# Splitting the first modulation unit of a two-layer transformer kernel into one half per chunk of the input

## Chip, cores, metric

One core of one Trainium2 chip runs the whole program. The metric is the device time of one execution in microseconds (us). Before the change three runs gave 2346.82, 2341.54 and 2345.47; the median is 2345.47 us.

## What is computed

The reference is a two-layer model on 512 latent rows and 256 context rows of width 2048, in float32. What matters here is its very beginning, the modulated norm that feeds layer 0:

```
shift, scale, gate = jnp.split((sc @ ada_w[i] + ada_b[i])[:, None, :], 3, axis=-1)
shift_c, scale_c, gate_c = jnp.split(scc @ ada_w[i] + ada_b[i], 3, axis=-1)
h = rmsnorm(x, norm_w[i]) * (1.0 + scale) + shift
hc = rmsnorm(xc, norm_w[i]) * (1.0 + scale_c) + shift_c
...
p_in, p_gate, c_q, c_kv, k_r, a_gate = split_cols(h @ w_in, EV_SIZES)
```

`sc` and `scc` are the SiLU of two vectors of length 2048, and `ada_w[i]` is 2048 x 6144. So before the first product `h @ w_in` can start, two things have to be there: the row norms of x (a sum of squares over all 2048 columns), and the shift and scale of the columns in question (a product with 2048 rows of `ada_w`).

## The kernel before

**Layout.** x and the context lie transposed: 16 chunks `xt[j]` of 128 columns (on the partitions) by 768 rows (512 latent, 256 context). Each float32 product is made of three products of split operands, high by high, low by high and high by low, with `wh`, `wl` the two parts of a weight and `h0h`, `h0l` those of an activation.

**First norm (L363 to L377).** SyncE issues the loads of all 16 chunks. ScalarE squares a chunk (L369, L372), VectorE adds it to one running sum `ssq0` (L374, 14 additions; the tile's name is `rb0`). Then TensorE sums over the partitions: `stat_mm` makes six one-column matmuls for `ssq0` and six for the last square `sq` (L375, L376, helper L247). `rstd_col` (L221 to L225) makes the reciprocal root, `rows` (L239 to L241) spreads it over the partitions: six diagonal tiles `dg`, six matmuls into `prs`, and two copies into `rb0`.

**Modulation units.** A unit `u` is 512 columns of `ada_w` for two chunks: in units 0 to 7 the columns are the shift of chunks 2u and 2u+1, then their scale. `ada_steps` (L134) works a unit off in steps. Each of four steps loads two tiles `at` of 512 KB and makes four matmuls into one PSUM tile `pa`, each with 32 columns of weights into its own 32 rows of `pa` (the trace shows each of them as two, so a step is x8). After the fourth VectorE transposes `pa` into `ga` (L147); a small matmul `pb` sums the parts (L150); four additions on VectorE write shift and scale into `av` (L131).

**A chunk.** `h_chunk` (L258) needs `av` and `rb0`. VectorE makes the factor `acf` (L264) and the product `ht` (L269), ScalarE the high part `h0h` (L271), VectorE the low part `h0l` (L272); first for the 512 latent rows, then for the 256 context rows. Each chunk then feeds five entries of a work list: four pairs (group g, block b), each six matmuls `px` (L360, 512 columns) and `pc` (L361, 256 columns) in alternation, and one of three matmuls `gkr` (L358).

**Order of the work.** TensorE runs in the order in which the code is written (`manual_schedule`); the other engines' order is set by the scheduler of the framework. The loop over e = 0 to 7 (L400) takes chunks 2e and 2e+1. From e = 1 on, the steps of unit e stand between entries of the work list by a table: after each step as many entries (`main_step`) as `PLAN = (0, 2, 3, 3, 2)` says. With ten entries in the list, the products of chunks 2e-2 and 2e-1 lie among the steps of unit e. The weight tiles come by `load_w` (L111) and `load_kr` (L389) every second e; all loads stand in one queue on SyncE. The `at` tiles share 11 buffers. When the loop is over, the evacuation and the next norm follow (L447 to L462), and from there on units 8 and up are worked off by VectorE, ScalarE and GpSimd beside the matmuls.

In PSUM the small tiles (`ps6`, `pa`, `prs`, `pb`) alternate between two banks. From L384 on one of the two holds `gkr`, and `pa` and `pb` of all later units share the other.

Of the kernel before, what the change touches and what calls it, by code (L numbers as in the profile page):

```python
# [29 lines left out]
V_GB, V_SINK, V_PS, V_QN, V_KVN, V_HN, V_FN, V_NW, V_AB = 0, 16, 32, 36, 40, 44, 52, 68, 132  # L30
# [8 lines left out]
def tile_hybrid_dit(ctx: ExitStack, tc: tile.TileContext, ts: dict, out: bass.AP, dbg=None, upto=99):  # L39
    nc = tc.nc  # L40
    T, V, S, G, DM = nc.tensor, nc.vector, nc.scalar, nc.gpsimd, nc.sync
# [44 lines left out]
    cst = opool(ctx, "cst")  # L86
    st = cst.tile([P, KC, 32], F32, name="st")
# [5 lines left out]
    vec = cst.tile([P, V_N], F32, name="vec")  # L93
# [31 lines left out]
    def ada_place(u, pb, n):  # L125
# [5 lines left out]
            V.tensor_tensor(a[sl, :, :n], pb[:, :n, b4::4].rearrange("p v b -> p b v"), ab[:, :, :n], op=ALU.add)  # L131
        av[u] = a

    def ada_steps(u, pp, tp, nb=3, nt=2):  # L134

        pa = pp.tile([P, 512], F32, name=f"pa{u}", tag="pm")
        for q in range(4):
            at = []
            for i in range(2):
                at.append(tp.tile([P, 2, 512], F32, name=f"at{u}_{q}_{i}", tag="ada", bufs=nb))  # L140
                DM.dma_start(at[i], ts["ada"][u, 2 * q + i].rearrange("p (k w) -> p k w", w=512))
            for qd in range(4):
                T.matmul(pa[32 * qd : 32 * qd + 32, :], st[:, 4 * q + qd, :], at[qd // 2][:, qd % 2, :],
                         start=q == 0, stop=q == 3, skip_group_check=True)
            if q == 3:
                tr = tp.tile([P, 16, 32], F32, name=f"ga{u}", tag="ga", bufs=1)
                V.transpose(tr.rearrange("p b r -> p (b r)"), pa)  # L147
                yield
                pb = pp.tile([32, 2, 16], F32, name=f"pb{u}", tag="pm")
                T.matmul(pb, fold, tr[:, :, 0:2].rearrange("p b v -> p v b"), start=True, stop=True)  # L150
                ada_place(u, pb, 2)
            yield
# [91 lines left out]
    def stat_mm(ps6, sq, nb, d, first=True, last=True):  # L244
        col = onesd[d]
        for b in range(nb):
            T.matmul(ps6[:, b : b + 1], sq[:, b * P : (b + 1) * P], col,  # L247
                     start=first and b == 0, stop=last and b == nb - 1, skip_group_check=True)
# [9 lines left out]
    def h_chunk(j, xt, rb, u0, layer, hh, hl, tp, vs=(0, 1), low=V):  # L258

        a = av[u0 + j // 2]  # L260
        i = j % 2
        nw = vec[:, V_NW + 32 * layer + 2 * j : V_NW + 32 * layer + 2 * j + 2]
        ac = tiny.tile([P, 2], F32, name="acf", tag="acf", bufs=2)
        V.scalar_tensor_tensor(ac, a[:, 2 + i, :], 1.0, nw, op0=ALU.add, op1=ALU.mult)  # L264
        n0 = PARTS[vs[0]].start
        t = tp.tile([P, PARTS[vs[-1]].stop - n0], F32, name="ht", tag="ht")
        for v in vs:
            sl = slice(PARTS[v].start - n0, PARTS[v].stop - n0)
            V.scalar_tensor_tensor(t[:, sl], xt[:, PARTS[v]], ac[:, v : v + 1], rb[v], op0=ALU.mult, op1=ALU.mult)  # L269
            if low is V:  # L270
                S.activation(hh[v], t[:, sl], AF.Identity, bias=a[:, i, v : v + 1], scale=1.0)  # L271
                V.scalar_tensor_tensor(hl[v], t[:, sl], a[:, i, v : v + 1], hh[v], op0=ALU.add, op1=ALU.subtract)  # L272
            else:
                S.activation(t[:, sl], t[:, sl], AF.Identity, bias=a[:, i, v : v + 1], scale=1.0)
                S.copy(hh[v], t[:, sl])
                low.tensor_tensor(hl[v], t[:, sl], hh[v], op=ALU.subtract)

# [57 lines left out]
    pp = ppool(esP, "ppA", px=4, pc=2, pm0=1, pm1=1)  # L335
# [13 lines left out]
    ae = opool(esE, "adaE", side="right")  # L349
# [14 lines left out]
    ps6 = pp.tile([P, 6], F32, name="ps6", tag="pm", bufs=2)  # L364
    ssq0 = sp.tile([P, NT], F32, name="rb0")
    for j in range(KC):
        DM.dma_start(xt[j], ts["xT"][j])
    NB, FIRST = 11, 2
    S.activation(ssq0, xt[0], AF.Square)  # L369
    for j in range(1, KC):  # L370
        sq = sp.tile([P, NT], F32, name="sq", tag="ht", bufs=2)
        S.activation(sq, xt[j], AF.Square)  # L372
        if j < KC - 1:
            V.tensor_tensor(ssq0, ssq0, sq, op=ALU.add)  # L374
    stat_mm(ps6, ssq0, 6, D, True, False)  # L375
    stat_mm(ps6, sq, 6, D, False, True)  # L376
    r6 = rstd_col(ps6, 6)  # L377
    first_unit = ada_steps(0, pp, ae, NB)
    for _ in range(FIRST):
        next(first_unit)  # L380
    rb0 = rows(r6, 6, pp, ssq0)
    for _ in first_unit:
        pass
    gx = [new_px(2) for _ in range(2)]  # L384
    gc = [new_pc() for _ in range(2)]
# [9 lines left out]

    wq = {}
    EARLY = 4
    PLAN = (0, 2, 3, 3, 2)
    with tc.manual_schedule(engines={mybir.EngineType.PE}):
        ht = Ring(sp, 2)  # L400
        for e in range(8):
            if e % 2 == 0:
                for g in range(2):
                    wq[g] = load_w(win[g, e // 2])
                wq[2] = load_kr(e // 2)
            if e:
# [63 lines left out]
    for kq in range(2):  # L470
        w = load_w(ts["ev_kr"][kq], 1024, 128)
# [77 lines left out]
    for pr in range(2):  # L549
# [11 lines left out]
        for b in range(2):  # L561
            t = ta("psg")
# [20 lines left out]
    pp = ppool(esP, "ppM", s2=2, pj=2, pm=2)  # L583
# [205 lines left out]
    first = out0_first()  # L789
# [90 lines left out]
    pp = ppool(esP, "ppO", px=4, pc=2, pm=2)  # L880
# [94 lines left out]
    for kq in range(8):  # L975
        w = load_w(ts["od_mv0"][kq], 544, 272)
# [740 lines left out]
def pack(inputs):  # L1717
# [8 lines left out]
    for l in range(2):  # L1726
        w = f["ada_w"][l]
        b = f["ada_b"][l]
        for e in range(8):
            cols = np.r_[256 * e : 256 * e + 256, 2048 + 256 * e : 2048 + 256 * e + 256]  # L1730
            ada.append((w, b, cols))
        for e in range(4):
            ada.append((w, b, np.r_[4096 + 512 * e : 4096 + 512 * e + 512]))
# [98 lines left out]
```

## Time and profile before

| | |
|---|---|
| median of three runs | 2345.47 us |
| the profiled execution, its own time | 2345.14 us |
| its span in the trace | 2343.4 us |
| TensorE busy (matmul) | 2238.1 us, 96% of the span |
| VectorE busy | 1488.9 us, 64% |
| ScalarE busy | 1041.4 us, 44% |
| first matmul at | 23.94 us |
| first product of a chunk (`px`) at | 41.82 us |
| end of the last `gkr` product of the loop | about 156.5 us |

A row of the timeline has the start in us, the time from the first to the end of the last of a run of like instructions, the engine, the line, the operation, output and input with shapes, and how many. In square brackets stands how long the engine had been idle and what ended it. PE is TensorE's matmul, PEld its weight load, DVE VectorE, ACT ScalarE, POOL GpSimd, SPq the queue of loads that SyncE issues.

### The profile page before, as it was taken

Reading aid. Unit: us, or ns where it says so; the run is one execution under the profiler, and the core shown is the slowest. Engines: PE = TensorE matmul, PEld = TensorE weight load, DVE = VectorE, ACT = ScalarE, POOL = GpSimd, SP = SyncE. Lnnn points to the kernel's source line nnn. Section 1 sums busy time; section 2 is a strip of 40 time slices with the busy share of each in tenths; the row PEclk is TensorE's granted clock in tenths of the full one; section 3 lists DMA queues with packets and bytes.
Section 4 is the critical chain, followed back from the end, with each engine's and each line's share of the span. In section 5 each row is a group of like instructions: output and inputs, shape, how many; then the busy total and the mean of one; then the engine's idle time right before and its main releaser. Section 6 shows DMA issues by size and latency. Waiting matters only on the chain.

```text
span 2343.4 us, 34744 instructions
## 1 busy us (share of the span) xinstructions
PE 2238.1 (96%) x12920; PEld 1902.8 (81%) x12920; DVE 1488.9 (64%) x2748; ACT 1041.4 (44%) x2054; POOL 459.0 (20%) x393
## 2 busy tenths in 40 slices
PE   5999998999999999999999999999999999999997
PEld 3678887778889999877888898998888877777886
DVE  5578888875476666777767722522555576778435
ACT  4234454443244444554224522222655557666433
POOL 0015565764200000026212200000000010003111
PEclk9999999999999999999999999999999999999998
DMA  9854554563311111255775322123233212113434
GB/s 383 323 197 161 171 185 140 202 205 123 99 57 48 59 52 64 91 186 198 241 248 178 116 95 82 64 73 114 99 99 97 99 62 72 64 55 126 135 113 140
DMA packets 118586, 311.27 MB, mean 133 GB/s; under 512 B 13676, under 2 KB 21356, under 8 KB 118416
## 3 DMA queue, kind: packets, MB, share of 16 engines
q1 hardware_dynamic: 111536, 281.73, 35.9%
q0 software_dynamic: 6880, 27.32, 3.0%
q8 instruction: 101, 1.65, 0.3%
q14 instruction: 69, 0.57, 0.1%
HBM read 279.37 MB, written 29.62 MB: 132 GB/s over the span
## 4 chain that ended last, share of the span: by engine, by line
PE 68%; DVE 9%; issue 4%; DMA 3%; POOL 2%; ACT 2%; DVEq 0%; SPq 0%; ACTq 0%; POOLq 0%
PE px L289 20%; PE px L302 11%; PE pj L619 5%; PE pc L291 5%; PE px L1418 5%; PE s L682 4%; PE pc L302 3%; PE om L725 3%; PE pj L639 2%; POOL acc L169 2%; DMA at<-in_ada_dram 2%; PE s L1418 2%; DVE acc L164 2%; PE po L1337 2%; DVE wl L109 2%
## 5 line engine op out<-in xcount | busy, mean ns | idle before, releaser
L109 DVE TENSOR_TENSOR wl<-wraw,wh 128x512 fp32r<-128x512 f32 (+2 forms) x556 | 431.9, 783 | 420.3 <-ACT wh L108 417.1
L108 ACT CAST wh<-wraw 128x512 fp32r<-128x512 f32 (+2 forms) x556 | 324.5, 589 | 594.7 <-PE pc L291 145.9
L169 POOL TENSOR_TENSOR acc<-acc,at 128x512 f32<-128x512 f32 x180 | 282.7, 1571 | 282.7 <-ACT at L167 272.9
L164 DVE SCALAR_TENSOR_TENSOR acc<-at,st,acc 128x512 f32<-128x512 f32 x240 | 250.3, 1043 | 52.1 <-DMA at<-in_ada_dram 48.3
L167 ACT ACTIVATE at<-at,st 128x512 f32<-128x512 f32 x180 | 130.0, 724 | 180.2 <-DVE acc L164 152.8
L302 PE MATMUL px<-wh,hxh 128*128 128x512 f32 (+2 forms) x512 | 174.4, 341 | 0.1
L302 PE MATMUL px<-wl,hxh 128*128 128x512 f32 (+2 forms) x512 | 173.7, 339 | 0.0
L302 PE MATMUL px<-wh,hxl 128*128 128x512 f32 (+2 forms) x512 | 173.6, 339 | 0.0
L289 PE MATMUL px<-h0h,wl 128*128 128x512 f32 x384 | 155.3, 404 | 11.7 <-DVE wl L109 11.7
L289 PE MATMUL px<-h0h,wh 128*128 128x512 f32 x384 | 156.0, 406 | 1.0 <-ACT wh L108 0.8
L289 PE MATMUL px<-h0l,wh 128*128 128x512 f32 x384 | 153.7, 400 | 0.0
L291 PE MATMUL pc<-h0h,wl 128*128 128x256 f32 x400 | 113.9, 285 | 0.0
L291 PE MATMUL pc<-h0h,wh 128*128 128x256 f32 x400 | 113.7, 284 | 0.0
L291 PE MATMUL pc<-h0l,wh 128*128 128x256 f32 x400 | 113.6, 284 | 0.0
L302 PEld LDWEIGHTS px<-wh,hxh 128*128 128x128 f32 x512 | 96.2, 188 | 12.8 <-ACT sz L1261 1.0
L302 PEld LDWEIGHTS px<-wl,hxh 128*128 128x128 f32 x512 | 96.3, 188 | 11.3
L302 PEld LDWEIGHTS px<-wh,hxl 128*128 128x128 f32 x512 | 96.2, 188 | 11.0
L289 PEld LDWEIGHTS px<-h0h,wl 128*128 128x128 f32 x384 | 73.5, 191 | 32.2 <-DVE wl L109 15.5
L289 PE MATMUL px<-zxh,wl 128*128 128x512 f32 x224 | 88.9, 397 | 3.6 <-DVE wl L109 3.6
L289 PE MATMUL px<-zxh,wh 128*128 128x512 f32 x224 | 89.6, 400 | 2.0 <-ACT wh L108 1.1
L289 PEld LDWEIGHTS px<-h0h,wh 128*128 128x128 f32 x384 | 73.9, 193 | 19.5 <-ACT wh L108 2.5
L289 PE MATMUL px<-hxl,wh 128*128 128x512 f32 x224 | 89.2, 398 | 0.0
(877 smaller groups left out, 6231.7 us busy)
## 6 DMA issues: line engine op xcount, KB each, us to landing
at<-in_ada_dram SPq DMA_DIRECT2D x256, 256.0 KB, 3.1
at<-in_ada_dram SPq DMA_DIRECT2D x64, 512.0 KB, 8.2
wraw<-in_od_in_dram SPq DMA_DIRECT2D x64, 512.0 KB, 3.5
wraw<-in_ev_in_dram SPq DMA_DIRECT2D x56, 512.0 KB, 4.1
wraw<-in_ev_out_dram SPq DMA_DIRECT2D x44, 512.0 KB, 4.5
wraw<-in_od_out_dram SPq DMA_DIRECT2D x36, 512.0 KB, 3.5
wraw<-in_od_oz_dram SPq DMA_DIRECT2D x32, 512.0 KB, 3.5
xt<-in_xT_dram SPq DMA_DIRECT2D x16, 384.0 KB, 7.5
```

The costliest lines, as they stand in the source:

```text
L108: S.copy(h, src)
L109: low.tensor_tensor(l, src, h, op=ALU.subtract)
L164: V.scalar_tensor_tensor(acc[0], at, st[:, kc, 0:1], acc[0], op0=ALU.mult, op1=ALU.add)
L167: S.mul(m, at, st[:, kc, 1:2])
L169: G.tensor_tensor(acc[1], acc[1], m, op=ALU.add)
L289: T.matmul(px[b], w_, Hx[kc][r_], start=s0, stop=s1)
L291: T.matmul(pc[b], w_, Hc[kc][r_], start=s0 and b == 0, stop=s1, skip_group_check=True)
L302: T.matmul(p_, h_, w_, start=s0, stop=s1, skip_group_check=True)
L619: T.matmul(t, w_, r_[:, sl], start=kc == 0 and n == 0, stop=kc == 3 and n == 2)
L682: T.matmul(s[:, c0 - k0 : c1 - k0], l_, r_[:, c0:c1], start=n == 0, stop=n == 4)
L725: T.matmul(o[:, :256], v_[:, 6 - nk + b, :], p_[:, b, :], start=b == 0 and n == 0, stop=b == nk - 1 and n == 2)
L1418: T.matmul(px[b], w_, Hs[kc][r_], start=first and i == 0 and n == 0, stop=last and i == len(kcs) - 1 and n == 2)
```

## The change

Four edits, all at the beginning of the program:

1. The first norm's running sum is cut into three parts. At chunk 5 and chunk 10 the sum so far goes through its six `stat_mm` matmuls, and a new sum begins with a copy of the square on VectorE; the last part, with the last square added, goes last. That makes 13 additions and 2 copies where 14 additions were, and 18 one-column matmuls where 12 were.
2. The columns of units are packed so that chunk 2u's shift and scale stand first, then those of chunk 2u+1. Unit 0 is worked off in two halves by the new `ada_half_steps`: each half has eight loads of 256 KB (rows of 1 KB where rows of 4 KB were), four steps of matmuls 256 columns wide, a transpose of 256 columns, a `pb`, and four additions into its half of `av[0]`.
3. Half 0 stands where the whole unit stood. Half 1 stands ahead of `h_chunk` of chunk 1, and the five work entries of chunk 0 are issued ahead of half 1 (`main_step` five times right after chunk 0 is made).
4. `PLAN` becomes (2, 2, 2, 2, 2). At e = 1 the list holds only chunk 1's five entries.

```diff
+    def ada_half_steps(u, hf, pp, tp, nb):
+        pa = pp.tile([P, 512], F32, name=f"pa{u}_{hf}", tag="pm")[:, :256]
+        for q in range(4):
+            at = []
+            for i in range(2):
+                at.append(tp.tile([P, 2, 512], F32, name=f"at{u}_{hf}_{q}_{i}", tag="ada", bufs=nb)[:, :, :256])
+                DM.dma_start(at[i], ts["ada"][u, 2 * q + i].rearrange("p (k w) -> p k w", w=512)[:, :, 256 * hf : 256 * hf + 256])
+            for qd in range(4):
+                T.matmul(pa[32 * qd : 32 * qd + 32, :], st[:, 4 * q + qd, :], at[qd // 2][:, qd % 2, :],
+                         start=q == 0, stop=q == 3, skip_group_check=True)
+            yield
+        tr = tp.tile([P, 8, 32], F32, name=f"ga{u}_{hf}", tag="gah", bufs=1)
+        V.transpose(tr.rearrange("p b r -> p (b r)"), pa)
+        pb = pp.tile([32, 2, 8], F32, name=f"pb{u}_{hf}", tag="pm")
+        T.matmul(pb, fold, tr[:, :, 0:2].rearrange("p b v -> p v b"), start=True, stop=True)
...
     for j in range(1, KC):
         sq = sp.tile([P, NT], F32, name="sq", tag="ht", bufs=2)
         S.activation(sq, xt[j], AF.Square)
-        if j < KC - 1:
-            V.tensor_tensor(ssq0, ssq0, sq, op=ALU.add)
-    stat_mm(ps6, ssq0, 6, D, True, False)
-    stat_mm(ps6, sq, 6, D, False, True)
+        if j in (5, 10):
+            stat_mm(ps6, acc, 6, D, first, False)
+            acc, first = su.tile([P, NT], F32, name="sqs", tag=f"sqs{j}"), False
+            V.tensor_copy(acc, sq)
+        else:
+            V.tensor_tensor(acc, acc, sq, op=ALU.add)
+    stat_mm(ps6, acc, 6, D, False, True)
+    esU.close()
     r6 = rstd_col(ps6, 6)
-    first_unit = ada_steps(0, pp, ae, NB)
-    for _ in range(FIRST):
-        next(first_unit)
+    halves = [ada_half_steps(0, hf, pp, ae, NB) for hf in range(2)]
+    for _ in range(2):
+        next(halves[0])
     rb0 = rows(r6, 6, pp, ssq0)
-    for _ in first_unit:
+    for _ in halves[0]:
         pass
...
-    PLAN = (0, 2, 3, 3, 2)
+    PLAN = (2, 2, 2, 2, 2)
...
             for j in (2 * e, 2 * e + 1):
+                if j == 1:
+                    for _ in halves[1]:
+                        pass
                 h_chunk(j, xt[j], [rb0[:, p] for p in PARTS], 0, 0, *([H0[j][i][:, p] for p in PARTS] for i in range(2)), ht)
...
+                if j == 0:
+                    for _ in range(5):
+                        main_step()
```

From the end of the loop on, the order on every engine is the same as before. Three places on TensorE are the ones that the prediction speaks of. The names: `pa<-at` is a step of a unit or half, `pb<-ga` its last small matmul, `prs` belongs to the row norms; the activations are numbered, `h0h_161` and `h0l_162` are chunk 0, 163 and 164 chunk 1, 165 and 166 chunk 2.

First, the way to the first product of chunk 0. Before, the last step of unit 0, then two steps of unit 1 (`pa_406`) ahead of the product:

```order
L143 MATMUL pa_289<-at_3_1_338,st 32x512 x2
L240 MATMUL prs<-dg,con 128x128 x2
L150 MATMUL pb_346<-ga_344,con 32x32
L143 MATMUL pa_406<-at_0_0_407,st 32x512 x2
L143 MATMUL pa_406<-at_0_1_409,st 32x512 x2
L143 MATMUL pa_406<-at_1_0_415,st 32x512 x2
L143 MATMUL pa_406<-at_1_1_417,st 32x512 x2
L360 MATMUL px<-h0h_161,wh 128x512
```

After the change, at the same place, nothing stands between the `pb` of half 0 (`pb_0`) and chunk 0:

```order
L143 MATMUL pa_0_302<-at_0_3_1_351,st 32x256 x2
L264 MATMUL prs<-dg,con 128x128 x2
L149 MATMUL pb_0_359<-ga_0_357,con 32x16
L384 MATMUL px<-h0h_161,wh 128x512
L385 MATMUL pc<-h0h_161,wh 128x256
```

The two steps of unit 1 have moved behind chunk 0's products, and the products follow the `pb` directly.

Second, from the end of half 1 to chunk 1, which in the kernel before has no counterpart (there chunk 1 was made together with chunk 0). After the change, on TensorE:

```order
L143 MATMUL pa_1_437<-at_1_3_0_462,st 32x256 x2
L143 MATMUL pa_1_437<-at_1_3_1_464,st 32x256 x2
L149 MATMUL pb_1_472<-ga_1_470,con 32x16
L167 MATMUL pa_487<-at_0_0_488,st 32x512 x2
L167 MATMUL pa_487<-at_0_1_490,st 32x512 x2
L384 MATMUL px<-h0h_163,wh 128x512
L385 MATMUL pc<-h0h_163,wh 128x256
L384 MATMUL px<-h0l_164,wh 128x512
```

Between the last step of half 1 and the first product that needs its result stand one `pb` and one step of unit 1.

Third, the end of unit 1. Before, on TensorE, from its `pb` (`pb_486`) to chunk 2; ahead of this piece three entries of chunk 1 stand between the last step and the `pb`:

```order
L150 MATMUL pb_486<-ga_466,con 32x32
L360 MATMUL px<-h0h_163,wh 128x512
L361 MATMUL pc<-h0h_163,wh 128x256
L360 MATMUL px<-h0l_164,wh 128x512
L361 MATMUL pc<-h0l_164,wh 128x256
L360 MATMUL px<-h0h_163,wl 128x512
L361 MATMUL pc<-h0h_163,wl 128x256
L358 MATMUL gkr<-h0h_163,kw_383 128x512
L358 MATMUL gkr<-h0l_164,kw_383 128x512
L358 MATMUL gkr<-h0h_163,kw_384 128x512
L143 MATMUL pa_546<-at_0_0_547,st 32x512 x2
```

After the change, from the last entry of chunk 1 to chunk 2:

```order
L382 MATMUL gkr<-h0h_163,kw_397 128x512
L167 MATMUL pa_487<-at_3_0_539,st 32x512 x2
L167 MATMUL pa_487<-at_3_1_541,st 32x512 x2
L174 MATMUL pb_549<-ga_547,con 32x32
L167 MATMUL pa_600<-at_0_0_601,st 32x512 x2
L167 MATMUL pa_600<-at_0_1_603,st 32x512 x2
L384 MATMUL px<-h0h_165,wh 128x512
```

The work list is empty when unit 1's last step is issued, so no products stand around its `pb`; one step of unit 2 is all that is left ahead of chunk 2. For units 2 to 7 the list holds ten entries again, and two entries follow each step and the `pb`.

More of the change, by code (lines that the diff above doesn't have):

```diff
@@ L132, in ada_place @@
         av[u] = a
+    def ada_half_steps(u, hf, pp, tp, nb):
[13 more added lines that the diff above has]
+        T.matmul(pb, fold, tr[:, :, 0:2].rearrange("p b v -> p v b"), start=True, stop=True)
+        if not hf:
+            av[u] = cst.tile([P, 4, 2], F32, name=f"av{u}")
+        for b4 in range(4):
+            sl = slice(32 * b4, 32 * b4 + 32)
+            ab = vec[sl, V_AB + 8 * u + 4 * hf : V_AB + 8 * u + 4 * hf + 4].rearrange("p (b v) -> p b v", v=2)
+            V.tensor_tensor(av[u][sl, 2 * hf : 2 * hf + 2, :], pb[:, :, b4::4].rearrange("p v b -> p b v"), ab, op=ALU.add)
+        yield
     def ada_steps(u, pp, tp, nb=3, nt=2):
@@ L263, in h_chunk @@
         ac = tiny.tile([P, 2], F32, name="acf", tag="acf", bufs=2)
-        V.scalar_tensor_tensor(ac, a[:, 2 + i, :], 1.0, nw, op0=ALU.add, op1=ALU.mult)
+        V.scalar_tensor_tensor(ac, a[:, 2 * i + 1, :], 1.0, nw, op0=ALU.add, op1=ALU.mult)
         n0 = PARTS[vs[0]].start
@@ L270, in h_chunk @@
             if low is V:
-                S.activation(hh[v], t[:, sl], AF.Identity, bias=a[:, i, v : v + 1], scale=1.0)
-                V.scalar_tensor_tensor(hl[v], t[:, sl], a[:, i, v : v + 1], hh[v], op0=ALU.add, op1=ALU.subtract)
+                S.activation(hh[v], t[:, sl], AF.Identity, bias=a[:, 2 * i, v : v + 1], scale=1.0)
+                V.scalar_tensor_tensor(hl[v], t[:, sl], a[:, 2 * i, v : v + 1], hh[v], op0=ALU.add, op1=ALU.subtract)
             else:
-                S.activation(t[:, sl], t[:, sl], AF.Identity, bias=a[:, i, v : v + 1], scale=1.0)
+                S.activation(t[:, sl], t[:, sl], AF.Identity, bias=a[:, 2 * i, v : v + 1], scale=1.0)
                 S.copy(hh[v], t[:, sl])
@@ L367, in tile_hybrid_dit @@
         DM.dma_start(xt[j], ts["xT"][j])
-    NB, FIRST = 11, 2
+    NB = 11
     S.activation(ssq0, xt[0], AF.Square)
+    esU = ExitStack()
+    su = opool(esU, "sums", side="right")
+    acc, first = ssq0, True
     for j in range(1, KC):
@@ L1729, in pack @@
         for e in range(8):
-            cols = np.r_[256 * e : 256 * e + 256, 2048 + 256 * e : 2048 + 256 * e + 256]
+            cols = np.concatenate([np.arange(P) + o + 256 * e for o in (0, 2048, P, 2048 + P)])
             ada.append((w, b, cols))
```

## Prediction

> **What bounds the kernel now.** I read the page first.
>
> ```profile
> span 2343.4 us, 34744 instructions
> PE 2238.1 (96%) x12920; PEld 1902.8 (81%) x12920; DVE 1488.9 (64%) x2748; ACT 1041.4 (44%) x2054; POOL 459.0 (20%) x393
> ```
>
> TensorE's matmuls fill 96%: what is idle on TensorE is what can be won, and a late start moves the rest. The change touches only the first 157 us, so the timeline of the startup comes next.
>
> ```profile
> 9.11 14.78 DVE L374 TENSOR_TENSOR rb<-rb,sq 128x768 f32<-128x768 f32 x14 [7.69 <-ACT sq L372]
> 23.94 2.72 PE L247 MATMUL ps<-od,rb 128*128 128x1 f32 x12 [23.94 <-DVE rb L374]
> 26.52 2.70 PE L247 MATMUL ps<-od,sq 128*128 128x1 f32 x12
> 29.15 1.93 PE L143 MATMUL pa<-at,st 128*32 128x512 f32 x8
> 29.26 0.16 DVE L221 TENSOR_SCALAR rs<-ps 128x6 f32<-128x6 f32 x1 [5.37 <-PE ps L247]
> 31.01 2.09 PE L240 MATMUL prs<-dg,con 128*128 128x128 f32 x8
> 32.97 2.36 ACT L108 CAST wh<-wraw 128x512 fp32r<-128x512 f32 x4 [3.31 <-DMA wraw<-in_ev_in_dram]
> 33.04 2.78 PE L143 MATMUL pa<-at,st 128*32 128x512 f32 x24
> 33.14 0.69 DVE L241 COPY rb<-prs 128x512 f32<-128x512 f32 x1
> 35.91 0.72 DVE L147 STREAM_TRANSPOSE ga<-pa 128x512 f32<-128x512 f32 x1 [1.88 <-PE pa L143]
> 37.33 0.28 PE L150 MATMUL pb<-ga,con 128*32 128x32 f32 x2
> 38.46 1.29 DVE L109 TENSOR_TENSOR wl<-wraw,wh 128x512 fp32r<-128x512 f32 x2
> 38.53 3.36 PE L143 MATMUL pa<-at,st 128*32 128x512 f32 x16 [0.93 <-PE pb L150]
> 41.82 0.80 PE L360 MATMUL px<-h0h,wh 128*128 128x512 f32 x1
> 44.07 0.39 PE L361 MATMUL pc<-h0h,wh 128*128 128x256 f32 x1 [1.46 <-ACT h0h L271]
> ```
>
> It reads as one chain: VectorE's sum, TensorE's 12 column matmuls (as 24 rows), the norm, unit 0's last step, its transpose, `pb`, then VectorE and ScalarE up to chunk 0 at 41.82. Note 38.53: two steps of unit 1 run on TensorE while VectorE makes chunk 0. The windows show what follows (busy of PE, PEld, DVE, ACT, POOL, then granted clock, DMA share, GB/s).
>
> ```profile
> 35.80:39.00 3.20, 1.41 (x16) 0.88 (x16) 2.21 (x7) 0.05 (x1) 0.00 (x0) 1.00 1.03 415
> 39.00:42.50 3.50, 3.50 (x17) 0.82 (x9) 3.50 (x9) 0.72 (x1) 0.00 (x0) 0.52 1.03 410
> 60.00:100.00 40.00, 40.00 (x239) 25.40 (x238) 18.23 (x46) 8.47 (x15) 0.00 (x0) 1.00 0.87 342
> ```
>
> From 44.07 TensorE is never idle in the loop but at its very end (below). So the loop can't be made shorter; only its start can come earlier, and any step moved behind that start adds its full time.
>
> **1. The head start: -4.1 us.** An addition takes 14.78/14 = 1.056. Thirteen make 13.73. A copy of 128x768 inside SBUF isn't in the trace; the nearest row is another one-input operation there:
>
> ```profile
> L162 DVE TENSOR_SCALAR acc<-at,st 128x512 f32<-128x512 f32 x1 | 0.5, 481 | 0.0
> ```
>
> 481 ns x 768/512 = 0.72 (bounds 0.48 and an addition's 1.06; I take 0.72, its row being the same kind of operation). So the last addition ends at 9.11 + 13.73 + 1.44 = 24.3 instead of 23.9, and only one group of six column matmuls is left (the other twelve run before 23.9, when TensorE has nothing else): the sums are there at 24.3 + 2.7 = 27.0 instead of 29.2: -2.2. Ahead of `prs` stand 9 of half 0's 16 matmuls; a step of 512 columns took 1.86 here (29.15 to 31.01), so 2.25 half steps take 2.1 and `prs` starts at 29.15: -1.85. Before, three steps stood between `prs` and the transpose (4.90 from 31.01 to 35.91); now 1.5 half steps do, and VectorE is what is late: `prs` to the copy 2.13, the copy 0.69, a `dg` 0.28 makes 3.1, so the transpose starts at 32.25: -3.65. Half as wide it takes 0.4 instead of 0.72, and one `acf` of 0.1 fewer is ahead of chunk 0. Chunk 0 starts at 37.7: -4.1 (bounds -2.6 to -4.6). Its weights cover: fewer bytes (2.1 MB, at 415 GB/s 5.05 us) are ahead of them, so the cast of 32.97 starts near 28. Rows of 1 KB at full queue aren't in the trace; at half the rate the half unit lands 5 us later, near 32, which is when the transpose was due: hidden, but the casts would then cost some 0.8. The wait of 44.07 moves along unchanged, since its chain on VectorE (two `wl`, `kw`, `h0l`, `ht`) is the same.
>
> **2. What moves behind the start: +4.9 us.** From the loop:
>
> ```profile
> 46.31 1.07 PE L143 MATMUL pa<-at,st 128*32 128x512 f32 x8
> 47.31 0.50 PE L360 MATMUL px<-h0h,wh 128*128 128x512 f32 x1
> 54.63 0.28 PE L150 MATMUL pb<-ga,con 128*32 128x32 f32 x2
> 54.84 0.50 PE L360 MATMUL px<-h0h,wh 128*128 128x512 f32 x1
> 56.78 1.92 PE L143 MATMUL pa<-at,st 128*32 128x512 f32 x16
> 58.64 0.50 PE L360 MATMUL px<-h0h,wh 128*128 128x512 f32 x1
> ```
>
> A step by itself takes 1.0 (46.31 to 47.31), two together 1.86, a `pb` 0.2. Half 1 is four steps of half the width in one block: 4 x 0.93/2 = 1.9, and its `pb` 0.2. Unit 1's first two steps, until now under VectorE's work at 38.53, come behind chunk 0: 2.0. In units 2 to 7 the pair of steps at the front is parted: 6 x 0.14 = 0.8. With the head start that is +0.8 already.
>
> **3. The new waits: +8.4 us.** Unit 7's end in the kernel before shows the chain from `pb` to the next chunk with only two entries of the list over it:
>
> ```profile
> 142.89 0.28 PE L150 MATMUL pb<-ga,con 128*32 128x32 f32 x2
> 145.67 0.49 PE L360 MATMUL px<-h0h,wh 128*128 128x512 f32 x1 [0.55 <-ACT h0h L271]
> 146.64 0.49 PE L360 MATMUL px<-h0l,wh 128*128 128x512 f32 x1 [0.18 <-DVE h0l L272]
> 147.26 0.39 PE L360 MATMUL px<-h0h,wl 128*128 128x512 f32 x1
> ```
>
> From `pb` to the chunk's third `px` 4.37 pass, set by VectorE and ScalarE (shift and scale, `ht`, `h0h`, `h0l`). Ahead of `pb` comes the transpose, 0.72 for 512 columns, 0.4 for 256, and 0.14 on either side of it.
>
> Half 1: from its last step 0.54 + 4.37 - 0.1 (one `acf`) = 4.8. TensorE has in it a `pb` 0.2, a step of unit 1 1.0 and the first two pairs of products 0.7: 2.9 idle. Unit 1: its list has run out, so 0.86 + 4.37 = 5.2 less the same 1.9: 3.3 idle. Units 2 to 6: two entries behind `pb` end 2.23 after it (145.12), one step 1.0, two pairs 0.7: 3.93 of 4.37, 0.44 idle, five times 2.2. Queued behind each of these waits is the rest of the loop on TensorE; nothing else can fill it, since the order is fixed.
>
> On SyncE's queue half 1's loads come in where unit 1's first ones stood, so unit 1's and the next weights' are put back by 2.1 MB, 5 us. Unit 1's last five tiles of 512 KB also wait for half 1's steps to free buffers, from 45 on (39.95 and chunk 0's entries, 5.0, as they take before from 44.07 to 50.1 without the step at 46.31); 2.6 MB at 415 GB/s take 6.3 and are there at 52. TensorE needs the last at unit 1's fourth step, near 58 (45 + 1.9 + 4.8, the rest of chunk 1's entries 4.3 and two steps), so I cost the loads at nothing; without those 6 us of cover they would add what they are late.
>
> **4. The clock: +3 us.** It fell to half after gaps:
>
> ```profile
> 165.60:168.40 2.80, 0.03 (x1) 0.03 (x1) 2.77 (x7) 0.21 (x1) 1.61 (x2) 1.00 0.64 195
> 168.40:172.10 3.70, 3.69 (x15) 3.41 (x16) 2.72 (x7) 1.45 (x2) 1.96 (x2) 0.56 0.40 153
> 241.00:244.20 3.20, 0.02 (x2) 0.00 (x1) 3.17 (x6) 1.35 (x3) 1.57 (x3) 0.95 1.08 357
> 244.20:250.40 6.20, 6.20 (x23) 5.71 (x24) 3.98 (x11) 1.66 (x3) 0.55 (x1) 0.50 0.65 231
> ```
>
> Two gaps of about 3 us were followed by 3.7 and 6.2 us at half; and 35.80:39.00, with 1.41 busy of 3.20 in pieces, by 3.5 at half. Ahead of chunk 0 TensorE will now be idle from the end of `pb` at 33.5 (37.6 - 4.1) to 37.7, so the half clock lasts until 41.2 to 43.9 (37.7 + 3.5 or 6.2); the dense products start at 39.95 (37.7 + 2.25): half of the stretch from there is lost, 0.6 to 2.0, and I take 1.3. The waits at half 1 and unit 1 are 3.5 to 4 us with 1.2 busy in pieces, emptier than 35.80:39.00. Each that drops the clock loses half of 3.5: 1.75 (up to 3.1). The wait of 1.46 ahead of 44.07 dropped nothing. These rows don't settle how little work is too little, so I take one of the two: 1.3 + 1.75 = 3.05.
>
> [...]
>
> **Sum.** -4.1 + 4.9 + 8.4 + 3.05 = +12.2. The profiled execution took 2345.14 (span 2343.4 and 1.7 around it), 0.3 under the median, which is nothing here: 2345.3 + 12.2 = 2357.5 us.
>
> **Rivals.**
>
> *The clock holds in both gaps.* A `pb` and a step stand in each gap, so no stretch without a matmul is longer than 0.9 (0.86 to `pb`, 0.7 to the step, 0.8 to the product), and the 1.46 ahead of 44.07 dropped nothing. Then 12.2 - 1.75 = +10.5: 2356. [...]
>
> *Later waits give it back.* The loop's end is followed by two waits of TensorE, 2.8 and 3.2 us (the windows 165.60 and 241.00), for VectorE, which by then also works on later units. If those units' loads and sums, not TensorE's products, set these waits, a later loop shortens them, and 1.85 and 3.1 of half clock behind them (half of 3.7 and 6.2) go too: up to 10.95 back, 2346.5, not slower. It decides from about 7.5 given back. Against it: VectorE runs in order, behind the chunks that are late themselves, and both waits begin with sums of TensorE's results.
>
> *Faster.* Without any wait of part 3 and any clock of part 4, and with the largest head start, -4.6 + 4.9 = +0.3 is left: 2345.6. To be faster by 4.7 chunk 0 would have to start 5.0 earlier still, near 32.2, which is before half 0's transpose. I see no row for it.
>
> *It doesn't do what it says:* a step of 256 columns takes as long as one of 512. Then half 1 costs 1.9 more and half 0 some 0.5: 2360.
>
> **Chances.** Forecast (one or both gaps drop the clock: 2357.5 to 2359.3) 0.50; clock holds 0.28; wide steps 0.07; given back 0.12; faster 0.03. About 0.2% (4.7 us) is what a measurement of this kernel tells from no change: slower 0.85, same 0.12, faster 0.03. Range: from 2349 (the clock holds, 10.5, less 2.0 for the ends of parts 1 and 3, and 4.8 given back) to 2363.5 (9.2 + 2.0 + 3.1 + 3.1 = +17.4, and 0.8 for the casts).
>
> **What would show it.** Chunk 0's first `px` near 37.7 (36.5 to 39.5); the sums at 27.0; at half 1's and unit 1's ends TensorE idle near 2.9 and 3.3 with ScalarE's `h0h` or VectorE's `h0l` as releaser; about 0.4 at the ends of units 2 to 6; a clock under 1 just behind 38 and behind at least one of the two waits; the last `gkr` near 168.5 instead of 156.5. I am wrong if the waits are there but the span isn't longer (given back), if chunk 0 starts ahead of 33, or if TensorE waits for `at` loads.

## The result and the profile after

The changed kernel took 2357.53 us (median of 4 runs, 2352.07 to 2361.29), the kernel before beside it 2343.51 us (4 runs, 2336.64 to 2346.82): a ratio of 1.006 with an interval of 1.0043 to 1.0077. The forecast was 2357.5, slower. The profiled execution is the shortest of the four: 2352.07 us.

```profile
span 2349.2 us, 34864 instructions
PE 2242.8 (95%) x12966; PEld 1901.2 (81%) x12966; DVE 1485.5 (63%) x2754; ACT 1040.8 (44%) x2054; POOL 463.1 (20%) x393
```

With the span 5.8 us longer, TensorE is busy 4.7 longer (2238.1 before). The timeline of the start and of the loop (start us, us, engine, line, operation, idle before and its releaser) tells where:

```profile
12.22 0.55 DVE L403 COPY sqs<-sq 128x768 f32<-128x768 f32 x1
26.29 0.16 DVE L245 TENSOR_SCALAR rs<-ps 128x6 f32<-128x6 f32 x1 [2.81 <-PE ps L271]
28.88 1.22 PE L264 MATMUL prs<-dg,con 128*128 128x128 f32 x4
32.29 0.69 DVE L265 COPY rb<-prs 128x512 f32<-128x512 f32 x1
33.09 0.44 DVE L147 STREAM_TRANSPOSE ga<-pa 128x256 f32<-128x256 f32 x1
38.30 0.80 PE L384 MATMUL px<-h0h,wh 128*128 128x512 f32 x1 [3.83 <-ACT h0h L295]
40.95 0.58 PE L385 MATMUL pc<-h0h,wh 128*128 128x256 f32 x1 [1.85 <-ACT h0h L295]
48.00 1.93 PE L143 MATMUL pa<-at,st 128*32 128x256 f32 x32
50.53 0.24 PE L149 MATMUL pb<-ga,con 128*32 128x16 f32 x2 [0.60 <-DVE ga L147]
51.55 1.06 PE L167 MATMUL pa<-at,st 128*32 128x512 f32 x8 [0.79 <-PE pb L149]
53.24 0.49 PE L384 MATMUL px<-h0h,wh 128*128 128x512 f32 x1 [0.62 <-ACT h0h L295]
61.33 1.06 PE L167 MATMUL pa<-at,st 128*32 128x512 f32 x8
63.26 0.28 PE L174 MATMUL pb<-ga,con 128*32 128x32 f32 x2 [0.86 <-DVE ga L171]
64.34 1.07 PE L167 MATMUL pa<-at,st 128*32 128x512 f32 x8 [0.81 <-PE pb L174]
66.03 0.58 PE L384 MATMUL px<-h0h,wh 128*128 128x512 f32 x1 [0.63 <-ACT h0h L295]
79.70 0.28 PE L174 MATMUL pb<-ga,con 128*32 128x32 f32 x2
79.91 0.50 PE L384 MATMUL px<-h0h,wh 128*128 128x512 f32 x1
80.72 0.39 PE L384 MATMUL px<-h0h,wl 128*128 128x512 f32 x1
83.08 0.49 PE L384 MATMUL px<-h0h,wh 128*128 128x512 f32 x1 [0.15 <-ACT h0h L295]
84.04 0.50 PE L384 MATMUL px<-h0l,wh 128*128 128x512 f32 x1 [0.18 <-DVE h0l L296]
84.66 0.40 PE L384 MATMUL px<-h0h,wl 128*128 128x512 f32 x1
158.41 0.28 PE L174 MATMUL pb<-ga,con 128*32 128x32 f32 x2
161.19 0.49 PE L384 MATMUL px<-h0h,wh 128*128 128x512 f32 x1 [0.55 <-ACT h0h L295]
```

Chunk 0 starts 3.5 us earlier (38.30, 41.82 before). Chunk 2 starts 7.4 later (66.03, 58.64 before), unit 7's `pb` 15.5 (158.41, 142.89 before), and with it chunk 14 (161.19, 145.67 before). In between stand the three small waits of half 1's end, the three of unit 1's end, and at the ends of units 2, 4 and 6 two short ones each, as at 83.08 and 84.04. The windows show the granted clock (us, busy of PE, PEld, DVE, ACT, POOL, then granted clock, DMA share, GB/s):

```profile
36.00:38.00 2.00, 0.00 (x0) 0.00 (x0) 1.96 (x5) 0.47 (x1) 0.00 (x0) 0.50 1.02 408
44.00:46.00 2.00, 2.00 (x8) 1.71 (x8) 0.00 (x0) 0.00 (x0) 0.00 (x0) 0.54 0.00 0
46.00:48.00 2.00, 2.00 (x12) 1.43 (x11) 0.00 (x0) 0.00 (x0) 0.00 (x0) 1.00 0.00 0
49.45:52.87 3.42, 1.79 (x22) 0.32 (x10) 2.36 (x8) 0.40 (x1) 0.00 (x0) 1.00 0.93 326
63.11:66.52 3.41, 1.83 (x12) 0.60 (x12) 2.96 (x11) 1.26 (x3) 0.00 (x0) 0.97 1.03 417
66.52:69.90 3.38, 3.38 (x11) 2.70 (x11) 2.36 (x5) 1.03 (x2) 0.00 (x0) 0.53 1.02 410
```

All of chunk 0 up to 46 ran at half clock (0.50 to 0.54), half 1's gap kept the full clock (1.00), unit 1's lost it (0.53 behind it). From where the records of the granted clock begin (near 32) to the program's last 20 us they show half clock only in stretches of 3.4, 6.8 or 10.2 us, always multiples of 3.4; the trace of before has 15 such pieces of 3.4 there, that of after 11.

### The profile page after: what moved, and what is told of

Its sections match the earlier page's. It is cut to its first block, busy times and chain, and to the rows that moved or that the text cites. A ratio compares the mean times of both kernels' runs of the same rounds, so it can differ in the third digit from the quotient of the medians.

```text
span 2349.2 us, 34864 instructions
## 1 busy us (share of the span) xinstructions
PE 2242.8 (95%) x12966; PEld 1901.2 (81%) x12966; DVE 1485.5 (63%) x2754; ACT 1040.8 (44%) x2054; POOL 463.1 (20%) x393
## 3 DMA queue, kind: packets, MB, share of 16 engines
q8 instruction: 101, 1.65, 0.3%
## 4 chain that ended last, share of the span: by engine, by line
PE 67%; DVE 9%; issue 3%; DMA 3%; ACT 2%; POOL 2%; DVEq 0%; ACTq 0%; POOLq 0%; SPq 0%
PE px L313 19%; PE px L326 11%; PE pj L656 5%; PE pc L315 5%; PE px L1455 5%; PE s L719 4%; PE pc L326 3%; PE om L762 3%; PE pj L676 2%; PE s L1455 2%; DMA at<-in_ada_dram 2%; PE po L1374 2%; POOL acc L193 2%; DVE wl L109 2%; PE tp L744 2%
## 5 line engine op out<-in xcount | busy, mean ns | idle before, releaser
L109 DVE TENSOR_TENSOR wl<-wraw,wh 128x512 fp32r<-128x512 f32 (+2 forms) x556 | 426.3, 774 | 417.5 <-ACT wh L108 412.8
L313 PE MATMUL px<-zxl,wh 128*128 128x512 f32 x224 | 89.5, 400 | 0.0
```

The costliest lines, as they stand in the source:

```text
L109: low.tensor_tensor(l, src, h, op=ALU.subtract)
L313: T.matmul(px[b], w_, Hx[kc][r_], start=s0, stop=s1)
```

## The experiments

The theory is the prediction's: the new order leaves TensorE waiting at the ends of half 1 and of the units, and the clock falls with it; the sums and the half steps themselves cost nothing. The first rival is that pieces of the change (half steps, 1 KB rows, the three-part sums) carry the loss; the second, that most of what the loop loses is given back behind it. The product at 161.19 (145.67 before), the first that needs unit 7, serves as the loop's end. It is chunk 14's first `px`; the expectations call it chunk 15's, wrongly, and mean this one.

**The kernels again.** First the changed kernel unchanged, for a second trace.

> The changed kernel once more, to tell what in its time is the order and what is the granted clock. Landmarks in the trace of the first profile: chunk 2's first product at 66.03 us (before 58.64), chunk 15's at 161.19 (before 145.67), so the loop ends 15.5 later. Theory (the order makes the loop longer, later work only shifts; how often the clock halves later on is chance): chunk 2 at 65 to 68, chunk 15 at 159 to 163, and the spans of the runs differ as (1 - granted clock) x span does; time about 12 to 15 over before. Rival (later waits give it back): the landmarks the same, and all spans near 2349, about 6 over before, with nothing left for the clock to explain.

2355.39 us (5 runs), ratio 1.0049 (1.0037 to 1.0061). The loop's end is at 162.00, +16.3; half clock from 38.3 and 65.6, 6.8 each (a `px` takes 0.63 there, 0.39 or 0.40 behind it). Of the five spans the shortest, 2350.9, has the highest granted clock (0.988) and the longest, 2355.6, the lowest (0.984), but they are 4.7 apart where (1 - clock) x span differs by 9.5; they do not all lie near 2349. And one more execution of the kernel before:

> The kernel before once more, for its trace: chunk 15 at 144.5 to 147.5 (145.67 in the first trace). If the first trace was a usual one, half-clock stretches stand behind the two waits of about 3 us at 169 and 244; elsewhere they may come and go.

Its loop's end is at 148.48, 2.8 later than in its first trace, outside what was expected: half clock here covers 43.8 to 50.6, dense products (0.63 a `px`, 0.39 behind it), instead of 39.3 to 42.7. Its span is 2343.7 all the same. Of the half clock expected behind the two waits near 169 and 244 only the second is there, from 248.7 on. So one trace of a loop's end carries some 3 us of luck, and the loop's loss is 14.5 between the means of two traces each (161.6 and 147.1).

**The order undone, the pieces kept.** On the changed kernel, half 1's steps go ahead of chunk 0's first product, into TensorE's idle time, and the plan is the former one:

```
-    PLAN = (2, 2, 2, 2, 2)
+    PLAN, PLAN1 = (0, 2, 3, 3, 2), (0, 3, 0, 3, 2)      # PLAN1 for e == 1
...
-                if j == 1:
-                    for _ in halves[1]:
-                        pass
...
-                    for _ in range(5):
-                        main_step()
+                    for n, _ in zip((0, 0, 0, 2, 0), halves[1]):
+                        for _ in range(n):
+                            main_step()
```

> Sums in three parts and unit 0 in halves stay; only the order on TensorE is another: half 1's steps stand ahead of chunk 0's products, two of chunk 0's entries cover its transpose, three of them and unit 1's steps cover the way to chunk 1, and units 2 to 7 have the old table. Theory (the loss is waits and parted steps that the order makes): no wait of TensorE over 1 us from chunk 0's second product on; chunk 2 at 57 to 59.5, chunk 15 at 144 to 147; time within 3 us of before, so 11 to 14 under the changed kernel. Rival (the halved unit is dear by itself: more and smaller loads, more steps, copies): chunk 15 at 152 or later, time 6 or more over before.

2341.10 us (12 runs), ratio 0.999 (0.9979 to 1.0). The whole loss is gone with both halves, the 1 KB rows and the parted sums still there: the first rival falls. The timeline of its start:

```profile
35.66 1.93 PE L143 MATMUL pa<-at,st 128*32 128x256 f32 x32 [0.95 <-PE pb L149]
38.55 0.49 PE L384 MATMUL px<-h0h,wh 128*128 128x512 f32 x1 [0.96 <-ACT h0h L295]
41.20 0.38 PE L385 MATMUL pc<-h0h,wh 128*128 128x256 f32 x1 [2.16 <-ACT h0h L295]
45.59 3.54 PE L167 MATMUL pa<-at,st 128*32 128x512 f32 x16 [0.79 <-PE pb L149]
```

Half 1's steps cost nothing at 35.66, where TensorE would only wait for VectorE's work. But chunk 2 comes at 61.28, not at 57 to 59.5, and the loop ends at 148.37, not at 144 to 147: TensorE was idle for 2.16 ahead of `pc`, where no wait over 1 us was expected, the clock was half from 42.5 on (0.50 in 42.50:45.90, 0.56 in 45.90:49.30), and two steps took 3.54 instead of 1.9.

**The sums alone.** The kernel before with the three-part sums and nothing else:

```
-        if j < KC - 1:
-            V.tensor_tensor(ssq0, ssq0, sq, op=ALU.add)
-    stat_mm(ps6, ssq0, 6, D, True, False)
-    stat_mm(ps6, sq, 6, D, False, True)
+        if j in (5, 10):
+            stat_mm(ps6, acc, 6, D, first, False)
+            acc, first = su.tile([P, NT], F32, name="sqs", tag=f"sqs{j}"), False
+            V.tensor_copy(acc, sq)
+        else:
+            V.tensor_tensor(acc, acc, sq, op=ALU.add)
+    stat_mm(ps6, acc, 6, D, False, True)
```

> The kernel before with the first norm's sums in three parts, nothing else. Theory: the sums are there 2.9 us earlier, but two steps of unit 1 stand ahead of chunk 0 and their loads come as late as before, so chunk 0's first product moves only from 41.82 to about 41.0 and chunk 15's from 145.67 to 145 (144 to 145.7): time 0 to 2 under before, not to be told from it. Rival (the sums set the start): chunk 0 at 39.5 or earlier, chunk 15 at 143.5, time 2 to 3 under before.

2343.11 us (11 runs), ratio 0.9997 (0.9988 to 1.0006).

```profile
36.14 4.50 PE L143 MATMUL pa<-at,st 128*32 128x512 f32 x16 [0.92 <-DVE av L131]
41.68 0.39 PE L361 MATMUL pc<-h0h,wh 128*128 128x256 f32 x1 [0.60 <-ACT h0h L271]
143.32 0.50 PE L360 MATMUL px<-h0h,wh 128*128 128x512 f32 x1 [0.55 <-ACT h0h L271]
```

`pc` moves by 2.39, from 44.07 to 41.68, and the loop's end by nearly the same 2.35, to 143.32, the rival's number. Chunk 0's first product, at 40.57, came as the theory had it (41.0; the rival's 39.5); the theory had overlooked that `pc` waits for VectorE, whose chain the sums shorten, however late TensorE is with unit 1's two steps. In the time this is too small to be told. And the changed kernel without them (the lines above taken back):

> The changed kernel with the first norm's sums as before (one running sum, two column products at its end), the halves and the order kept. Theory (the parted sums are worth what they were in the kernel before, 2.35 us, at the start of the chain to chunk 0): chunk 0's first px near 40.7 (38.3 with them), chunk 15's first px at 163 to 164.5, time 2356 to 2361. Rival (the extra matmuls and the copy of the parted sums are part of the loss): chunk 0 at 38.5 or earlier, chunk 15 at 160.5 or earlier.

2359.37 us (4 runs), ratio 1.0067 (1.0046 to 1.0089); chunk 0 at 40.85, as expected and 2.55 later, so what the sums win lies in the start of the chain. The loop's end came at 166.17, 1.7 later than the end of the expected span. One reason is in half 1's gap, built as in the changed kernel:

```profile
53.38 0.24 PE L149 MATMUL pb<-ga,con 128*32 128x16 f32 x2 [0.60 <-DVE ga L147]
54.41 1.07 PE L167 MATMUL pa<-at,st 128*32 128x512 f32 x8 [0.79 <-PE pb L149]
56.10 0.80 PE L384 MATMUL px<-h0h,wh 128*128 128x512 f32 x1 [0.62 <-ACT h0h L295]
```

The same waits to 0.01 us, but the product behind them takes 0.80 (0.49 at 53.24 above): here the clock was half from 56.2 to 59.6 (0.63 for the `px` at 58.34). With this the delay against the changed kernel grows from 2.85 (half 1's block at 50.85, 48.00 there) to 3.78 (unit 1's `pb` at 67.04, 63.26 there). The other reason is the half clock at chunk 2, 6.8 us long here (69.8 to 76.6) and 3.4 in the changed kernel's first trace: behind it the delay is 5.07 (unit 2's `pb` at 84.77, 79.70 there).

**The plan alone put back.** The changed kernel with the former plan for units 2 to 7:

```
+    PLAN, PLAN1 = (0, 2, 3, 3, 2), (2, 2, 2, 2, 2)      # PLAN1 for e == 1
```

> The changed kernel with the old table (0, 2, 3, 3, 2) for units 2 to 7; unit 1 keeps (2, 2, 2, 2, 2). Theory: up to chunk 2 as the changed kernel (66 to 67), then 14.5 a unit as before instead of 15.6, so chunk 15 at 154 to 156.5 and the time 4 to 6 under the changed kernel, 8 to 10 over before. Rival (the table costs nothing, the loss lies all ahead of chunk 2): chunk 15 at 160 or later.

2348.84 us (7 runs), ratio 1.0023 (1.0012 to 1.0033); the loop's end at 155.05.

```profile
64.74 2.10 PE L167 MATMUL pa<-at,st 128*32 128x512 f32 x12 [0.80 <-PE pb L174]
67.07 1.05 PE L167 MATMUL pa<-at,st 128*32 128x512 f32 x4 [0.23 <-DMA at<-in_ada_dram]
78.65 0.28 PE L174 MATMUL pb<-ga,con 128*32 128x32 f32 x2
152.27 0.28 PE L174 MATMUL pb<-ga,con 128*32 128x32 f32 x2
```

The pair of steps at unit 2's front fills unit 1's gap, and no clock drops there in this trace (0.39 a `px` from 68.51 on); one step waits 0.23 for its load. From unit 2's `pb` to unit 7's five units take 14.72 each, as before (14.71, 54.63 to 142.89 over six), against 15.74 in the changed kernel (79.70 to 158.41). The even plan alone is 6.1 us at the loop's end (161.19 to 155.05): 5.1 from there on and 1.0 ahead of unit 2's `pb` (1.4 counted from unit 1's `pb`, to which this kernel came 0.4 later).

**Half 1's wait covered.** The changed kernel with one entry of chunk 0 first and two behind each of half 1's last two steps, so that the work that is there stands over the transpose and the chain:

```
-                    for _ in halves[1]:
-                        pass
+                    for n, _ in zip((0, 0, 0, 2, 2), halves[1]):
+                        for _ in range(n):
+                            main_step()
...
-                    for _ in range(5):
-                        main_step()
+                    main_step()
```

> The changed kernel, but only one of chunk 0's five entries stands ahead of half 1's steps; two follow its last step and two its pb. At unit 1's end the scheduler now puts two low parts of weights (1.3 us on VectorE) ahead of chunk 2's factors. Theory: the idle time around half 1's pb (0.6, 0.8 and 0.6, and 0.8 more at the low parts) is gone, unit 1's end waits up to 1.3 longer; chunk 2 at 62.5 to 65.5, chunk 15 at 158 to 161. Rival (the waits there are not for want of work but for loads or the clock): chunk 2 at 66 or later.

2356.0 us (4 runs), ratio 1.005 (1.0034 to 1.0065).

```profile
48.92 0.24 PE L149 MATMUL pb<-ga,con 128*32 128x16 f32 x2
61.67 0.28 PE L174 MATMUL pb<-ga,con 128*32 128x32 f32 x2 [0.86 <-DVE ga L171]
62.69 0.69 DVE L109 TENSOR_TENSOR wl<-wraw,wh 128x512 fp32r<-128x512 f32 x1
63.44 0.69 DVE L109 TENSOR_TENSOR wl<-wraw,wh 128x512 fp32r<-128x512 f32 x1
62.76 1.65 PE L167 MATMUL pa<-at,st 128*32 128x512 f32 x8 [0.81 <-PE pb L174]
65.59 0.79 PE L384 MATMUL px<-h0h,wh 128*128 128x512 f32 x1 [1.19 <-ACT h0h L295]
```

Half 1's wait (0.60 + 0.79 + 0.62) is gone: unit 1's `pb` comes 22.6 us behind chunk 0's first product (39.11), against 25.0 and 24.6 in the two traces of the changed kernel. Yet chunk 2 starts only 0.4 earlier than in the first of these, between what the theory and the rival had said, and the loop ends at 161.00. Chunk 0 came 0.8 later in this trace, and at unit 1's end two low parts of weights (`wl`) now stand on VectorE ahead of chunk 2's `ht`, as expected: from `pb` to chunk 2 pass 3.92 instead of 2.77. The clock also fell inside this gap (63.3; the step takes 1.65, in the changed kernel's first trace 1.07), but behind the step TensorE still waits 1.19 for `h0h`, so the gap is not longer for that. Half 1's wait is thus worth some 2 us where it stands; this order loses them again at VectorE, and in the time nothing shows.

**The clock held up.** Thrown-away products (plain float32, 512 columns; they take 0.87 us each, and for the first two kernels I had assumed half of it) in the idle places around chunk 0's start. On the changed kernel nine, then four, ahead of chunk 0:

```
+                    for _ in range(9):      # 4 in the second kernel
+                        T.matmul(gkr, ident, xt[1][:, :NX], start=True, stop=True, skip_group_check=True)
```

> The changed kernel with nine matmuls of 128x512 ahead of chunk 0's first product, in TensorE's idle 3.8 us between half 0's pb and that product; their result is thrown away by the first gkr matmul. Theory (the half clock behind that gap is TensorE's own idleness): no stretch at half clock between 36 and 46, chunk 0's 22 products behind the wait for pc (40.95 to 48.00 in the changed kernel, 7.05) take 4.9 to 5.3, and chunk 15 starts about 2 earlier, at 158.5 to 160.5. Rival (the clock does not look at TensorE's idle time here): half clock from 36 to 46 as before, chunk 15 at 161 or later.

2358.34 us (5 runs), ratio 1.006 (1.0046 to 1.0073). The nine ran to 43.1, so chunk 0 began 4.8 late (43.13), but at full clock (0.39 or 0.40 a `px`): from its first `pc` (43.77) to half 1's block (48.55) 4.8 us, where the changed kernel takes 7.05 (40.95 to 48.00). In this trace such products held the clock up at chunk 0, as the theory had it, but the loop's end, at 161.64, is where the rival had it.

> The changed kernel with four thrown-away products (0.86 us each) instead of nine ahead of chunk 0, from 35.7 to about 39.2. Theory (chunk 0's half clock is 2 to 3 us of the loop's +15, the nine ran too long): no half clock between 36 and 50, chunk 0's products done in about 5 us, chunk 15's first px at 158 to 159.7 (161.19 and 162.00 without, 161.64 with nine). Rival (the clock falls in the idle 1.5 us between px and pc anyway, or what chunk 0 wins is lost in half 1's wait): 160.5 to 162. Time 2352 to 2357 by the theory, as the changed kernel (2355 to 2358) by the rival.

2357.18 us (4 runs), ratio 1.0062 (1.0042 to 1.0083); the loop's end at 160.94, the rival's number. Two windows of it:

```profile
36.90:40.30 3.40, 1.24 (x5) 0.32 (x3) 2.82 (x6) 1.17 (x2) 0.00 (x0) 0.97 0.68 263
40.30:43.70 3.40, 3.40 (x11) 3.05 (x12) 0.44 (x1) 0.00 (x0) 0.00 (x0) 0.53 0.00 1
```

The four ran from 34.13 to 37.62, and with the 2.16 us idle between `px` and `pc` the clock dropped all the same, behind 3.40 us with 1.24 busy. Covering the first gap and not the second shows no gain.

On the filled order, products ahead of `px` and between `px` and `pc`: 2 and 4, then 1 and 2:

```
+    def spin(n):
+        for _ in range(n):
+            T.matmul(gkr, ident, xt[1][:, :NX], start=True, stop=True, skip_group_check=True)
...
+                if opening and n == 0:      # between px and pc of chunk 0's first entry
+                    spin(4)                 # 2 in the second kernel
...
                     for n, _ in zip((0, 0, 0, 2, 0), halves[1]):
+                        if n:
+                            spin(2)         # 1 in the second kernel
```

> The reordered version (label fill) with two thrown-away matmuls ahead of chunk 0's first product and four between it and the second, where TensorE was idle for 0.96 and 2.16 us. There the clock was half from 42.5 to 49.3. Theory: no half clock in the loop, chunk 15 at 144.5 to 146 instead of 148.4; time 3 to 5 under before. Rival (what is gained in the loop does not reach the end): chunk 15 as said, time as label fill, within 1 us of it.

2344.42 us (11 runs), ratio 1.0002 (0.9993 to 1.0012). The two steps take 1.93 again (46.11), but `pc` comes 1.5 late (42.72), and the loop's end at 147.19, where 144.5 to 146 was expected and a time 3 to 5 under before.

> Kernel with the halves and the parted sums, half 1's steps in TensorE's idle time ahead of chunk 0, and now one thrown-away product ahead of chunk 0's first px and two between px and pc (0.86 us each), so that they end at about 41.1 and push nothing back; nothing else is changed against the kernel with the too long row of such products (2 and 4). Theory (the half clock behind chunk 0's start is what kept the filled order from its 144 to 147): no stretch below clock 0.9 before 60, pc near 41.2, chunk 15's first px at 144.5 to 146 (148.37 with the half clock and no such products, 147.19 with too many). Rival (the products in between come out as late as the half clock would make them): 147 or later. On the time: if what is won in the loop reaches the end in full, 2338 to 2340; if the stretches of half clock behind the loop are dealt anew and eat it, 2341 to 2345, not told from before.

2340.98 us (12 runs), ratio 0.9992 (0.9982 to 1.0002).

```profile
35.68 3.62 PE L143 MATMUL pa<-at,st 128*32 128x256 f32 x32 [0.95 <-PE pb L149]
41.75 0.68 PE L392 MATMUL pc<-h0h,wh 128*128 128x256 f32 x1
44.12 0.24 PE L149 MATMUL pb<-ga,con 128*32 128x16 f32 x2
45.15 1.92 PE L167 MATMUL pa<-at,st 128*32 128x512 f32 x16 [0.79 <-PE pb L149]
146.29 0.49 PE L389 MATMUL px<-h0h,wh 128*128 128x512 f32 x1 [0.55 <-ACT h0h L295]
```

This time the clock fell ahead of half 1's steps (half clock from 36.0 to 39.4: 3.62 for 1.93), and not again in the loop; the loop ends just outside the 144.5 to 146 expected. From `pc` to the loop's end 104.5 us pass here and 104.5 in the kernel with more such products; before it was 101.6, and with the sums alone 101.6. The 2.9 more are a `pb`, the 0.79 wait and the 1.92 of two steps, which before ran under VectorE's work. The sums win 2.4 and the halves cost 2.9: even in the best order that I found, the halves win nothing. No kernel here beats the one before by what can be told.

**What lies behind the loop.** The second rival can be tried on all 13 profiles. From each the span less the time of the loop's end is what follows, and the granted clock's records give the pieces of 3.4 us at half clock in it (ahead of the program's last 20 us):

```
kernel                    loop end   behind it   pieces of 3.4 us
before                     145.67     2197.7      14
before, again              148.48     2195.2      13
sums alone                 143.32     2193.4      11
order undone               148.37     2187.5       8
  with 2 and 4 products    147.19     2195.8      13
  with 1 and 2 products    146.29     2194.0      11
former plan                155.05     2191.9       9
half 1's wait covered      161.00     2195.5      12
after                      161.19     2188.0       7
after, again               162.00     2188.9       8
  with nine products       161.64     2190.7       9
  with four products       160.94     2192.2      11
  without the sums         166.17     2192.7      12
```

A straight line, 2178.2 + 1.35 for each piece, fits all 13 within 1.7 us (correlation 0.95). The late kernels stand on the same line as the early ones: a term of its own for the late seven comes to +0.2 with a standard error of 0.7. So no wait behind the loop gives time back: the profiled executions of before and after differ there by 9.7 us, of which 9.5 are, by the line's 1.35, seven pieces fewer at half clock. Whether a later loop makes such pieces fewer is not settled: the early six kernels had 11.7 on average, the late seven 9.7, and each ranges over 5 or more. The loop's loss of 14.5 stands beside times whose means differ by 14.5 (4 runs each) and 11.9 (changed kernel again, 5 runs against 25).

## Why the prediction was right, and where it was not

- **The head start: -3.5, forecast -4.1.** The sums were there at 26.25 (forecast 27.0), because the additions began at 7.94 in this trace and not at 9.11. A copy took 0.55, not 0.72, but VectorE then waited 0.44 for ScalarE's next square, 0.99 in all. In the second trace the sums were there at 26.96, and chunk 0 still started at 38.28. For `prs` to its copy took 3.4 (28.88 to 32.29; 2.67 in the second trace) instead of 2.13, because half steps stand between the `prs` pairs, so the transpose came at 33.09, not 32.25. The step that failed took a duration from a place where nothing stood between the rows.
- **Half 1: right.** The block took 1.93 (forecast 1.9), and 3.31 passed from its end to chunk 1 (49.93 to 53.24; the forecast 4.8 to the third `px`, less 1.59 from the first to the third, is 3.2). Steps of 256 columns cost half (1.93 for these four, 1.92 for two of 512 at 56.78 before): that rival is out.
- **Unit 1's end: right.** From the end of its last step (61.33 + 1.06) to chunk 2 3.64 passed; the forecast 5.2 less the same 1.59 is 3.6.
- **The wait of units 2 to 6: mis-sized.** "0.44 idle" and 0.14 for the parted pair make 0.58 a unit; it was 1.0 (15.74 against 14.71), and the former plan takes all of it away (14.72). The term took its chain, 4.37 from `pb` to the third `px`, from unit 7's end. At units 3 and 5 the chain is that long (4.36, from 95.68 to 100.04), and such a unit takes 0.7 more than before (15.38, 14.66 before). At units 2, 4 and 6, where new weights are made ready, ScalarE casts a part of `kw` ahead of `h0h`:

```profile
81.78 0.62 ACT L108 CAST kw<-kw 128x512 fp32r<-128x512 f32 x1 [0.18 <-PE gkr L382]
82.31 1.12 ACT L295 ACTIVATE h0h<-ht,av 128x512 fp32r<-128x512 f32 x2
```

  So `h0h` starts 2.61 behind `pb`, where at unit 3 it starts 2.00 behind it (97.68), and 4.96 pass to the third `px` (79.70 to 84.66), exactly as in the kernel before (69.28 to 74.24). But before, two steps of the next unit ran in this stretch, and now one does; the other comes later and adds its time, and such a unit takes 1.2 more (15.98, 14.79 before). Little of this shows as idle time, only 0.15 and 0.18. The rest is pace: a chunk's first two pairs of products run as VectorE and ScalarE hand over `h0h` and `h0l`, 1.58 to the third `px` (83.08 to 84.66) where a later entry takes 0.81 (79.91 to 80.72). Over five units that is 2.2 more than forecast.
- **The clock: right in kind.** Chunk 0 lost some 2.2 (4.8 at full clock with the nine products, 7.05 without), a little over the upper end of 0.6 to 2.0; I took 1.3. Of the two gaps one dropped it, as taken. That it was the second and not the first was luck as far as the rows tell: windows of 1.79 and 1.83 busy in 3.4 (above) went one way and the other, and half 1's identical gap dropped it in the kernel without the sums (0.80 for the product behind it, 0.49 here).
- **The sum.** At the loop's end +15.5 in this pair of traces (14.5 between the means of two each), not +12.2: 0.6 of head start and 0.9 of chunk 0's clock are missing in it and 2.2 of the units, while unit 1's drop of the clock and the rest came out some 0.4 less. The last `gkr` came at 171.6, not at 168.5. That the time agrees to 0.1 us is therefore partly luck: the loop lost more than the sum said, and the medians differ by 14.0, where 12.2 was forecast; the sum started from 2345.3, and the kernel before took 2343.51 beside the changed one.
- **Given back: false** as a mechanism. The wait of 2.78 behind the loop became three of 0.29, 1.74 and 0.64, 2.67 together. The one of 3.18 ahead of 244.20 became 2.40, but it is 2.40 too in the kernel with the order undone, whose loop ends at 148.37. **Loads:** none of `at`'s was waited for in the changed kernel's loop, as costed.

## What to carry to other kernels

Where one engine is full and runs in a fixed order, bringing its start forward wins nothing if the work that stood in the idle time before it has to be done behind it (here chunk 0 came 3.5 us earlier and the loop's end 14.5 later): count what the idle time was holding. Moving products ahead of steps takes them away from the place where they covered another engine's chain, and here the price was paid at every turn of the loop (1.0 us a unit), also as a slower pace of the first products and not only as idle time. Measure that chain at every turn: here it was 0.6 longer at every second one (4.96 and 4.36). A single trace of this kernel is good to some 3 us at a place (145.67 and 148.48 for one loop's end) and some 10 at the end (2187.5 to 2197.7 for what follows); compare places in the program, and more than one profile.

## What was not expected of the hardware

- In the traces of before and after the half clock comes in pieces of 3.4 us (15 and 11 of them ahead of the last 20 us). In the line through the 13 profiles a piece goes with 1.35 us; with 7 to 14 of them behind the loop they account for most of the scatter of what follows it (correlation 0.95). That they make most of the scatter of the times (2336.8 to 2349.6 us for the kernel before in one set of 17 runs) is not shown: in the three sets of 25, 15 and 17 runs of that kernel the correlation of span and mean granted clock is only -0.23, -0.46 and -0.51.
- With a gap of 2.16 us between products the clock dropped in two kernels (to 0.50 with the order undone, to 0.53 with four products ahead of chunk 0), and with 2.15 in the second trace of the kernel before (0.63 a `px` behind it). A wait of 1.46 in its first trace didn't drop it (1.00 in 43.90:46.00), and gaps of over 3 us with pieces of work in them went either way (1.00 in half 1's, 0.53 behind unit 1's in the changed kernel).
- A plain float32 product of 512 columns takes 0.87 us at full clock (four from 34.13 to 37.62), against 0.23 from one `gkr` to the next (171.17 to 171.40) in the kernel's own type.
